# A two-layer hybrid mixer kernel: conditioning loads issued ahead, held subtracts, and six products in the second layer's front

## The chip, the cores and the metric

The kernel runs on one core of one Trainium2 chip. The metric is the device time of one execution in microseconds (us). Before the change it is 1586.25 us, the median of three runs (1586.24 to 1587.02). The engines are called by their short names: PE (TensorE, matmuls), DVE (VectorE), ACT (ScalarE), POOL (GpSimd) and SP (SyncE, which here only issues loads).

## The reference, cut to what matters

256 latent tokens and 256 context tokens of 1024 channels go through two layers. Each layer normalizes, scales and shifts its input by a conditioning vector, projects it once, feeds three mixers from the columns, merges them, and adds an MLP.

```
c_act = silu(c); cc_act = silu(c_ctx)
for l in range(2):
    sh1, sc1, g1, sh2, sc2, g2 = split(c_act @ w_ada[l] + b_ada[l], 6)      # 6144 columns
    ...                                                                      # the same for the context
    h  = rms_norm(x,  norm1[l]) * (1 + sc1)  + sh1
    hc = rms_norm(xc, norm1[l]) * (1 + sc1c) + sh1c
    u_f, dn_qkv, dn_z, dn_ab, da_q, da_k, da_v, gates = split_columns(h @ w_in[l])
    # A: Fourier mixing of u_f; B: bidirectional gated DeltaNet of dn_qkv (conv, silu, chunked delta rule);
    # C: differential attention; merged by sigmoid(gates), projected by w_o
    x = x + g1 * y
    x = x + g2 * squared_relu_mlp(rms_norm(x, norm2[l]) * (1 + sc2) + sh2)
    ...                                                                      # context: layer 0 only
return rms_norm(x, final_norm)
```

## The kernel before, in words

Activations lie channel-major: a tile holds 128 channels by tokens, and k counts the eight channel tiles. Each weight is split into a high and a low part (`whi`, `wlo`) in a rounded 32-bit format, and so is each activation (`hh`, `hl`). One product of 128 output channels is, for each k, three matmuls (`mm3`): high by high, low by high, high by low. A weight chunk is loaded (`raw`), copied by ACT into `whi`, and subtracted by DVE or POOL into `wlo` (`load_w`, L243 to L256).

The program is written with a tile framework that fixes the order on each engine's queue ahead of time: each instruction has a priority, by default its place in the program, and an instruction that the planner holds ready goes ahead of a later one. `Weave.chain` moves work of the mixers to places that are counted in PE's time. A buffer that is used again makes the writer wait for its last reader.

**Front 0** (`front0`, from L1241) prepares layer 0. It forms the square sums of both streams (L1309 on), the norm's row by `norm_rows` (L390: a reciprocal root in small steps, L381 to L387; four diagonal tiles `nd`, L402, that PE turns into rows; copies to `r`), and the conditioning. The first two groups of conditioning columns (shift and scale, eight tiles each) are computed in two ways. For the last NP = 3 tiles of each group PE multiplies (`matvec`): sixteen loads `wn` of 128 x 384 through four buffers. For the others DVE reduces transposed rows (`Rows.step`, L336: two reductions of 1024 elements a row, one for the latent and one for the context vector); the rows come two at a time through a ring of two slots (tile `wv`), and a slot's next load waits until its reductions are done.

Then eight steps follow in the order KO of k. A step finishes the conditioning of its k (two rows, L340, and `mod_gain`, L450), modulates both streams (`modulate`, L453: DVE's product L458, ACT's `hh` L459, ACT's shift L463, and POOL's subtract L464) and adds k to the open products (`step_of`). The products join by JOIN: the gates' 16 columns, then DeltaNet's query and key of head 0, two Fourier gates (C_GF), and DeltaNet's value. A product that joins late catches up on the steps done. All five full-width subtracts of these products are put on POOL by their calls (L1327 to L1331). MV says how many k of `matvec` are done at each step.

**Front 1** (`front1`, L1403) does the same for layer 1, where the conditioning is already there. Three products run along: the gates and DeltaNet's key and value of head 0. It modulates the eight k of the latent stream, then the eight of the context; the context's norm is finished between them. The subtracts of the weights of all twelve DeltaNet chunks of layer 1 alternate between POOL and DVE (`turn_dn`).

Behind each front `mixer` runs the DeltaNet pair of heads 0 and 1 (`dn_pair`): a product, copies by ACT, five taps of a convolution (DVE, L632), tanh, then transposes on PE. Products made in the front are taken from `pre` and not computed again. The Fourier branch follows.

```
places of the loops   KO = [0, 1, 2, 5, 6, 7, 3, 4]      JOIN = [0, 0, 0, 1, 2, 7]
                      MV = [4, 2, 2, 0, 0, 0, 0, 0]      NP = 3
```

Of the kernel before, what the change touches and what calls it, by code (L numbers as in the profile page):

```python
# [19 lines left out]
P = 128  # L20
# [25 lines left out]
NP = 3  # L46
MV = [4, 2, 2, 0, 0, 0, 0, 0]
KO = [0, 1, 2, 5, 6, 7, 3, 4]
JOIN = [0, 0, 0, 1, 2, 7]
# [132 lines left out]
def body(tc, A, dbg=None):  # L182
# [58 lines left out]
    turn_dn = [0]  # L241

    def load_w(l, n, pair=None, eng=V):  # L243
        if l == 1 and n < C_U:

            eng = (G, V)[turn_dn[0] % 2]
            turn_dn[0] += 1
        r = raw_tile(A["wck"][l, n])
        if pair is None:
            hi = wp.tile([P, 1024], F32R, tag="whi", name="whi")  # L250
            lo = wp.tile([P, 1024], F32R, tag="wlo", name="wlo")
        else:
            hi, lo = pair[:, 0], pair[:, 1]
# [20 lines left out]
    def split(src, hi, lo):  # L274
        S.copy(hi, src)  # L275
        V.tensor_tensor(out=lo, in0=src, in1=hi.bitcast(F32), op=ALU.subtract)  # L276
# [35 lines left out]
    class Rows:  # L312
# [15 lines left out]
        def step(self, k=1):  # L328
            for _ in range(k):
# [4 lines left out]
                for v in range(m):  # L334
                    junk = self.pool.tile([P, 1024], F16, tag="junk", name="junk")
                    V.tensor_tensor_reduce(out=junk, in0=r, in1=self.cb[:, v], scale=0.5, scalar=0.0, op0=ALU.mult, op1=ALU.add,  # L336
                                           accum_out=ada[l][:, n, v:v + 1])
# [52 lines left out]
    def norm_rows(ps, rs, pool, pr=None, later=None):  # L390
# [850 lines left out]
    def front0(mp, dp, job, gate_weights):  # L1241
# [5 lines left out]
        pair = lambda pool, tag, dt=F32R: pool.tile([P, 2, 1024], dt, tag=tag, name=tag)  # L1247
        crw = pair(mp, "oD", F32)[0:1].rearrange("p a b -> p (a b)")
# [23 lines left out]
        def wide():  # L1272
            return st.tile([P, 1024], F32, tag="sq", name="sq", bufs=3)

        def add(out, a, b):
            V.tensor_tensor(out=out, in0=a, in1=b, op=ALU.add)

        W = 128 * NP
        pa = [bank("pd") for _ in range(2)]
        mv = [0]  # L1280

        def matvec(m):
            for _ in range(m):
                k = mv[0]
                if k < KT:
                    for i in range(2):
                        r = mp.tile([P, 512], F32, tag="gt", name="wn", bufs=4)[:, :W]
                        nc.sync.dma_start(r, A["wn"][k][:, i * W:(i + 1) * W])
                        PE.matmul(pa[i][0:2, :W], cT[:, k], r, start=k == 0, stop=k == KT - 1)
# [15 lines left out]
        for s in range(2):  # L1305
            tot = st.tile([P, L], F32, tag="mt", name="tot", bufs=3)
            for i in range(2):
                q = wide()
                S.activation(q, x0[s][i].rearrange("p a b -> p (a b)"), AF.Square)  # L1309
                add(q[:, 0:512], q[:, 0:512], q[:, 512:1024])  # L1310
                if i == 0:
                    add(tot, q[:, 0:L], q[:, L:512])
                else:
                    add(q[:, 0:L], q[:, 0:L], q[:, L:512])
                    add(tot, tot, q[:, 0:L])
# [10 lines left out]
        jobs, late = [], [lambda: job("gates", gate_weights(), "pc", 16),  # L1326
                          lambda: job(("dn", 0, 0), load_w(0, C_DN, None, G), "pg"),  # L1327
                          lambda: job(("dn", 0, 1), load_w(0, C_DN + 4, None, G), "pg"),
# [184 lines left out]
```

## Time and profile before

| what | value |
|---|---|
| median of three runs | 1586.25 us |
| time of the profiled execution | 1584.71 us |
| its span, first to last instruction | 1582.6 us |
| PE busy | 1517.0 us, 96% |
| PE weight loads busy | 1305.2 us, 82% |
| DVE busy | 1166.3 us, 74% |
| ACT busy | 735.4 us, 46% |
| POOL busy | 145.0 us, 9% |
| moved by DMA | 215.31 MB, mean 136 GB/s |

Busy times are of one profiled execution. The span is cut into 40 slices of 39.6 us for the rows of tenths. A timeline row merges equal neighbours; its columns are start, length, engine, line, operation, written tile and read tiles, shapes, and count, with the idle time before it and what ended that. A window's row gives each engine's busy time and count, the clock granted to PE as a share of 2.4 GHz, the mean busy share of the DMA engines, and what they moved.

### The profile page before, as it was taken

The page shows a single profiled execution, that of the slowest core. Times are in us where ns is not written, and L with a number is a line of the kernel's source. Part 1 is how long each engine was busy: PE and PEld are TensorE (multiplying, and loading weights), DVE is VectorE, ACT ScalarE, POOL GpSimd, SP SyncE. Part 2 cuts the span into 40 slices and gives each one's busy share as a digit, 9 for nine tenths or more (in the row PEclk, how much of TensorE's full clock was granted, in tenths as well). Part 3 has the DMA queues.
Part 4 walks back from the last instruction along what each step waited for, and adds up shares of the span by engine and source line. Part 5 has one row for each costly group of instructions (what it writes and reads, how often), then busy time and mean ns, then how long its engine had stood idle before and what let it go on. Part 6 is the DMA issues. An engine that isn't in the chain of part 4 may idle for free. (4 is left out here: it accounts for less than half of the span.)

```text
span 1582.6 us, 26109 instructions
## 1 busy us (share of the span) xinstructions
PE 1517.0 (96%) x10114; PEld 1305.2 (82%) x10114; DVE 1166.3 (74%) x2246; ACT 735.4 (46%) x1527; POOL 145.0 (9%) x173
## 2 busy tenths in 40 slices
PE   5899999999999999999999998899999999999997
PEld 2588888777888878888888888888988899999997
DVE  8787774768789797867676755776777886877765
ACT  3475533676532233423223233575457644555543
POOL 3400100011000012000000004001111100100001
PEclk9999999999999999999999999899999999999998
DMA  7532124211257573566566542141332135655662
GB/s 237 192 97 67 35 75 124 82 48 35 80 187 226 189 237 109 164 193 195 181 196 186 186 148 86 56 150 48 111 103 68 42 106 186 188 175 184 190 185 93
DMA packets 64461, 215.31 MB, mean 136 GB/s; under 512 B 7281, under 2 KB 12305, under 8 KB 64081
## 3 DMA queue, kind: packets, MB, share of 16 engines
q1 hardware_dynamic: 58178, 201.96, 40.7%
q10 hardware_dynamic: 5184, 7.21, 1.4%
q0 software_dynamic: 976, 4.48, 1.0%
q8 instruction: 79, 1.29, 0.4%
q14 instruction: 44, 0.36, 0.1%
HBM read 209.42 MB, written 4.20 MB: 135 GB/s over the span
## 5 line engine op out<-in xcount | busy, mean ns | idle before, releaser
L254 ACT CAST whi<-raw 128x1024 fp32r<-128x1024 f32 x277 | 290.5, 1050 | 220.6 <-PE pg L158 98.5
L255 DVE TENSOR_TENSOR wlo<-raw,whi 128x1024 fp32r<-128x1024 f32 x269 | 329.7, 1226 | 80.1 <-ACT whi L254 71.3
L158 PE MATMUL pg<-hh,whi 128*128 128x512 f32 (+1 forms) x856 | 304.0, 355 | 0.2
L158 PE MATMUL pg<-hh,wlo 128*128 128x512 f32 (+1 forms) x856 | 302.9, 354 | 0.5 <-DVE wlo L255 0.5
L158 PE MATMUL pg<-hl,whi 128*128 128x512 f32 (+1 forms) x856 | 303.1, 354 | 0.0
L336 DVE CUSTOM_DVE_ANT_0 junk<-raw,cb 128x1024 f16<-128x1024 f32 x128 | 157.0, 1227 | 57.8 <-DMA raw<-in_wt 56.3
L158 PEld LDWEIGHTS pg<-hh,whi 128*128 128x128 f32 x856 | 162.7, 190 | 20.6 <-issue 0.8
L158 PEld LDWEIGHTS pg<-hl,whi 128*128 128x128 f32 x856 | 162.8, 190 | 19.5 <-issue 0.8
L158 PEld LDWEIGHTS pg<-hh,wlo 128*128 128x128 f32 x856 | 162.7, 190 | 19.1 <-DVE wlo L255 0.7
L158 PE MATMUL pg<-a,whi 128*128 128x256 f32 (+1 forms) x448 | 107.5, 324 | 0.1
L435 POOL TENSOR_TENSOR acc<-acc,sq 128x256 f32<-128x256 f32 x36 | 38.1, 1067 | 661.7 <-ACT sq L433 661.7
L632 DVE SCALAR_TENSOR_TENSOR cy<-cu,conv,cy 128x512 f32<-128x512 f32 (+1 forms) x96 | 69.3, 723 | 30.3 <-ACT cy L630 29.0
L158 PEld LDWEIGHTS pg<-a,whi 128*128 128x128 f32 x448 | 75.8, 188 | 7.7 <-DVE a L276 0.8
L158 PE MATMUL pg<-a,wlo 128*128 128x256 f32 (+1 forms) x224 | 72.1, 322 | 0.0
L878 ACT ACTIVATE gt<-pg 128x256 f32<-128x256 f32 (+1 forms) x43 | 21.0, 488 | 102.6 <-PE pg L158 99.3
L158 PE MATMUL pd<-a,whi 128*128 128x512 f32 (+1 forms) x224 | 56.7, 334 | 0.1
L158 PE MATMUL pa<-hh,whi 128*128 128x512 f32 (+1 forms) x152 | 54.5, 358 | 1.0 <-ACT cy L630 0.9
L158 PE MATMUL pa<-hh,wlo 128*128 128x512 f32 (+1 forms) x152 | 54.0, 355 | 0.0
L158 PE MATMUL pa<-hl,whi 128*128 128x512 f32 (+1 forms) x152 | 53.6, 353 | 0.0
L1235 DVE TENSOR_TENSOR mr<-mr 128x512 f32<-128x512 f32 (+1 forms) x64 | 35.4, 555 | 23.6 <-ACT mr L1234 23.6
L158 PE MATMUL pg<-whi,hh 128*128 128x256 f32 (+1 forms) x160 | 50.9, 318 | 0.7 <-DVE q L996 0.5
L158 PE MATMUL pg<-wlo,hh 128*128 128x256 f32 (+1 forms) x160 | 50.1, 314 | 0.0
(444 smaller groups left out, 3611.4 us busy)
## 6 DMA issues: line engine op xcount, KB each, us to landing
raw<-in_wck SPq DMA_DIRECT2D x280, 512.0 KB, 3.6
raw<-in_wt SPq DMA_DIRECT2D x80, 512.0 KB, 3.6
wv<-in_wt SPq DMA_DIRECT2D x10, 512.0 KB, 4.1
wn<-in_wn SPq DMA_DIRECT2D x16, 192.0 KB, 3.7
x<-in_xin SPq DMA_DIRECT2D x4, 512.0 KB, 8.2
spill<-gt ACTq DMA_DIRECT2D x8, 256.0 KB, 3.9
cb<-crow POOLq DMA_DIRECT2D x2, 1024.0 KB, 7.0
merged<-spill ACTq DMA_DIRECT2D x8, 256.0 KB, 4.6
```

Source lines behind the costliest of these rows:

```text
L158: ins = self.pe.matmul(out, a, b, start=start, stop=stop)
L254: S.copy(hi, r)
L255: eng.tensor_tensor(out=lo, in0=r, in1=hi.bitcast(F32), op=ALU.subtract)
L336: V.tensor_tensor_reduce(out=junk, in0=r, in1=self.cb[:, v], scale=0.5, scalar=0.0, op0=ALU.mult, op1=ALU.add, accum_out=ada[l][:, n, v:v ...
L435: G.tensor_tensor(out=self.acc[s], in0=self.acc[s], in1=q, op=ALU.add)
L632: V.scalar_tensor_tensor(out=y3, in0=u[:, 0:ns, j:j + L], scalar=conv[:, f, j:j + 1], in1=y3, op0=ALU.mult, op1=ALU.add)
L878: S.activation(th, ps[:, :n], AF.Tanh, scale=0.5)
L1235: V.tensor_tensor(out=t, in0=t, in1=t, op=ALU.mult)
```

## The change

In front 0, four tiles of each conditioning group are PE's instead of three, and all sixteen `wn` loads (now 128 x 512) are issued before the norm, each into a buffer of its own: tiles that the later chunk stage of the mixer uses. The loads of x come before the first two rows. The pieces of the square sums are added up less on DVE and more in PE's accumulation. Two products are opened before the norm. Reductions and low-part subtracts that are called after `norm_rows` are ordered behind its last diagonal on DVE's queue (`hold`, `behind`). No subtract is on POOL any more, neither of weights nor of `modulate`. The order of steps and joins is new. In front 1, six products run along the latent stream and four along the context, three of them with weights in tiles of their own.

```diff
-NP = 3
-MV = [4, 2, 2, 0, 0, 0, 0, 0]
-KO = [0, 1, 2, 5, 6, 7, 3, 4]
-JOIN = [0, 0, 0, 1, 2, 7]
+NP = 4
+MV = [5, 3, 0, 0, 0, 0, 0, 0]
+KO = [0, 1, 4, 5, 6, 7, 2, 3]
+JOIN = [0, 0, 1, 2, 3, 4]
...
-    turn_dn = [0]
+    hold = [None]
+
+    def behind(ins):
+        if hold[0] is not None:
+            tc.add_manual_dep(ins.ins, hold[0].ins.name, mybir.DependencyInfo(mybir.DependencyClass.NoSync, mybir.DependencyReason.DATA), reason="behind")
 
     def load_w(l, n, pair=None, eng=V):
-        if l == 1 and n < C_U:
-
-            eng = (G, V)[turn_dn[0] % 2]
-            turn_dn[0] += 1
...
-        eng.tensor_tensor(out=lo, in0=r, in1=hi.bitcast(F32), op=ALU.subtract)
+        behind(eng.tensor_tensor(out=lo, in0=r, in1=hi.bitcast(F32), op=ALU.subtract))
...                                     # the same in split() and for the reductions of Rows.step
-    def norm_rows(ps, rs, pool, pr=None, later=None):
+    def norm_rows(ps, rs, pool, pr=None, later=None, nd=None):
...
-            d = pool.tile([P, P], F32, tag="nd", name="nd", bufs=2)
-            V.tensor_scalar(out=d, in0=one32, scalar1=y[:, t:t + 1], scalar2=None, op0=ALU.mult)
+            d = pool.tile([P, P], F32, tag="nd", name="nd", bufs=2) if nd is None else nd[:, t * P:(t + 1) * P]
+            ins = V.tensor_scalar(out=d, in0=one32, scalar1=y[:, t:t + 1], scalar2=None, op0=ALU.mult)
...
+        return ins
@@ front0
                 nc.sync.dma_start(x0[s][i], A["xin"][s][:, 4 * i:4 * i + 4])
-            if s == 0:
-                aw.fill()
+        aw.fill()
...
+        jobs = [job("gates", gate_weights(), "pc", 16), job(("dn", 0, 0), load_w(0, C_DN), "pg")]
         W = 128 * NP
...
+        places = [(mp, "gt", 4)] * 4 + [(dp, "U32", 3), (dp, "dec", 3)] * 3 + [(dp, "gq", 2)] * 2 + [(dp, t_, 1) for t_ in ("rh", "rl", "T32", "state")]
+        wn = []
+        for k in range(KT):
+            for i in range(2):
+                pool, tag, bufs = places.pop(0)
+                wn.append(pool.tile([P, 512], F32, tag=tag, name="wn", bufs=bufs)[:, :W])
+                nc.sync.dma_start(wn[-1], A["wn"][k][:, i * W:(i + 1) * W])
...                                     # matvec: its loads and their four buffers go
-            tot = st.tile([P, L], F32, tag="mt", name="tot", bufs=3)
+            qs = []
             for i in range(2):
-                q = wide()
+                q = wide() if s + i < 2 else dp.tile([P, 1024], F32, tag="C32", name="sq")
                 S.activation(q, x0[s][i].rearrange("p a b -> p (a b)"), AF.Square)
-                add(q[:, 0:512], q[:, 0:512], q[:, 512:1024])
...                                     # and the adds of the halves into tot
+                V.tensor_tensor(out=q[:, 0:512], in0=q[:, 0:512], in1=q[:, 512:1024], op=ALU.add)
+                qs += [q[:, 0:L], q[:, L:512]]
             for t in range(2):
-                PE.matmul(sums[:, 2 * s + t:2 * s + t + 1], tot[:, t * P:(t + 1) * P], oneD[:, 0:1], start=True, stop=True)
-            if s == 0:
-                aw.step()
-        norm_rows([sums[:, i:i + 1] for i in range(4)], r_, st)
+                for i, q in enumerate(qs):
+                    PE.matmul(sums[:, 2 * s + t:2 * s + t + 1], q[:, t * P:(t + 1) * P], oneD[:, 0:1], start=i == 0, stop=i == 3)
+        aw.step()
+        hold[0] = norm_rows([sums[:, i:i + 1] for i in range(4)], r_, st, nd=dp.tile([P, 512], F32, tag="vn", name="nd"))
...
-                          lambda: job(("dn", 0, 1), load_w(0, C_DN + 4, None, G), "pg"),
-                          lambda: job((C_GF, 1), load_w(0, C_GF + 1, pair(st, "wu"), G), "pa"),
-                          lambda: job((C_GF, 0), load_w(0, C_GF, pair(mp, "oD"), G), "pa"),
-                          lambda: job(("dn", 0, 2), load_w(0, C_DN + 8, pair(st, "wv"), G), "pd")]
+        late = [lambda: job(("dn", 0, 1), load_w(0, C_DN + 4), "pg"),
+                lambda: job((C_GF, 1), load_w(0, C_GF + 1, halves(pair(st, "wu"))), "pa"),
+                lambda: job((C_GF, 0), load_w(0, C_GF, halves(pair(mp, "oD"))), "pa"),
+                lambda: job(("dn", 0, 2), load_w(0, C_DN + 8, (wide(F32R), wide(F32R))), "pd")]
...
-                modulate(0, xv, r_, ma, 0, s, k, st, G)
+                modulate(0, xv, r_, ma, 0, s, k, st)
@@ front1
-        jobs = [job("gates", gate_weights(), "pc", 16)]
-        jobs += [job(("dn", 0, i), load_w(1, C_DN + 4 * i), t_) for i, t_ in ((1, "pg"), (2, "pd"))]
-        for s in range(2):
-            for k in range(KT):
-                modulate(1, x1, r1, ma, 0, s, k, cp_)
-                step_of(jobs, k, s * L, L, X=hs[1])
...
+        with tc.tile_pool(name="st1", bufs=1, reuse_waits="tile") as st:
+            pairs = [[st.tile([P, 1024], F32R, name=f"w{i}{c}") for c in "hl"] for i in range(3)]
+            both = [job("gates", gate_weights(), "pc", 16)]
+            both += [job(("dn", 0, i), load_w(1, C_DN + 4 * i), t_) for i, t_ in ((1, "pg"), (2, "pd"))]
+            lat = [job(("dn", 0, 0), load_w(1, C_DN, pairs[0]), "pg"), job((C_GF, 0), load_w(1, C_GF, pairs[1]), "pa")]
+            both.append(job(("dn", 1, 1), load_w(1, C_DN + 5, pairs[2]), "pa"))
+            for s in range(2):
+                for k in range(KT):
+                    modulate(1, x1, r1, ma, 0, s, k, cp_)
+                    step_of(both if s else both + lat, k, s * L, L, X=hs[1])
...
```

## Rows read from the trace of the kernel before

**Rows 1.** The page: PE's row of busy tenths in 40 slices.
```profile
PE   5899999999999999999999998899999999999997
```
**Rows 2.** Table by windows, front 0.
```profile
0.00:7.30 7.30, 3.50 (x4) 1.49 (x5) 2.44 (x8) 1.50 (x2) 3.69 (x12) 1.00 0.72 155
7.30:13.30 6.00, 3.66 (x6) 1.00 (x4) 4.15 (x9) 4.44 (x8) 0.00 (x0) 1.00 1.02 416
13.30:25.40 12.10, 1.00 (x4) 0.92 (x4) 12.06 (x19) 4.00 (x5) 6.45 (x3) 1.00 0.66 240
...
35.80:82.90 47.10, 41.01 (x167) 25.76 (x166) 33.16 (x59) 21.21 (x43) 20.83 (x18) 1.00 0.56 186
```
**Rows 3.** Timeline of front 0, 16 to 36 us.
```profile
16.82 5.92 POOL L255 TENSOR_TENSOR wlo<-raw,whi 128x1024 fp32r<-128x1024 f32 x2 [2.15 <-ACT whi L254]
...
17.98 2.55 DVE L1276 TENSOR_TENSOR tot<-sq 128x256 f32<-128x256 f32 x1
20.46 2.82 DVE L1276 TENSOR_TENSOR sq<-sq 128x512 f32<-128x512 f32 x1
...
24.35 0.41 DVE L1276 TENSOR_TENSOR sq<-sq 128x256 f32<-128x256 f32 x1
...
28.29 2.27 DVE L383 TENSOR_SCALAR rne<-rne 128x4 f32<-128x4 f32 x1
...
35.77 0.64 PE L158 MATMUL pc<-hh,wab 128*16 128x512 f32 x2
```
**Rows 4.** Timeline of layer 1's front and what follows it.
```profile
974.64 2.32 DVE L387 SCALAR_TENSOR_TENSOR rny<-rnp,rny 128x2 f32<-128x2 f32 x1
...
1016.23 2.33 DVE L530 SCALAR_TENSOR_TENSOR ge<-ge,ge 128x32 f32<-128x32 f32 x1
...
1019.22 1.12 PE L166 MATMUL pc<-kc,cy 128*128 128x128 f32 x4 [3.65 <-DVE cy L637]
```
**Rows 5.** Table by windows, layer 1's front and the convolutions behind it.
```profile
981.70:988.10 6.40, 3.99 (x32) 3.05 (x31) 6.40 (x10) 2.80 (x6) 5.25 (x8) 0.93 0.27 84
988.10:993.80 5.70, 5.70 (x27) 5.07 (x28) 4.27 (x20) 1.84 (x6) 0.00 (x0) 0.50 0.26 92
993.80:1005.60 11.80, 11.79 (x102) 10.82 (x100) 6.52 (x16) 4.48 (x11) 0.00 (x0) 0.99 0.00 0
...
1014.40:1021.60 7.20, 2.34 (x11) 1.57 (x10) 7.20 (x13) 4.40 (x16) 2.90 (x3) 0.74 0.25 71
1021.60:1030.00 8.40, 8.40 (x51) 7.84 (x51) 6.60 (x27) 4.97 (x14) 0.27 (x4) 0.81 0.16 49
```
**Rows 6.** Groups by line on DVE (busy us, mean ns); modulates on the timeline.
```profile
L336 DVE CUSTOM_DVE_ANT_0 junk<-wv,cb 128x1024 f16<-128x1024 f32 x20 | 28.2, 1412 | 2.0 <-DMA wv<-in_wt 1.8
...
L255 DVE TENSOR_TENSOR wlo<-raw,whi 128x1024 fp32r<-128x1024 f32 x2 | 2.4, 1214 | 0.0
...
L336 DVE CUSTOM_DVE_ANT_0 junk<-raw,cb 128x1024 f16<-128x1024 f32 x128 | 157.0, 1227 | 57.8 <-DMA raw<-in_wt 56.3
...
34.26 0.88 DVE L458 SCALAR_TENSOR_TENSOR mt<-x,ma,r 128x256 f32<-128x256 f32 x2 [0.35 <-ACT r L405]
...
996.96 1.27 DVE L461 SCALAR_TENSOR_TENSOR hl<-mt,ada,hh 128x256 fp32r<-128x256 f32 x3
```
**Rows 7.** Timeline: the last square of front 0.
```profile
14.30 1.06 ACT L1309 ACTIVATE sq<-x 128x1024 f32<-128x1024 f32 x1 [0.34 <-DMA x<-in_xin]
```
**Rows 8.** Timeline of PE in front 0.
```profile
26.37 5.24 PE L158 MATMUL pd<-wn,cT 128*2 128x384 f32 x8
...
79.40 0.39 PE L158 MATMUL pg<-hh,whi 128*128 128x512 f32 x1
79.63 0.40 PE L158 MATMUL pg<-hh,wlo 128*128 128x512 f32 x1
...
82.97 0.41 PE L166 MATMUL pd<-kc,ab 16*128 16x16 f32 x4
```
**Rows 9.** Waits of PE, 35 to 115 us: total, times, longest.
```profile
PE pc L158 <- POOL hl L464: 2.1, 3, 0.9
```

More of the change, by code (lines that the diff above doesn't have):

```diff
@@ L252, in load_w @@
         else:
-            hi, lo = pair[:, 0], pair[:, 1]
+            hi, lo = pair
         S.copy(hi, r)
-        eng.tensor_tensor(out=lo, in0=r, in1=hi.bitcast(F32), op=ALU.subtract)
+        behind(eng.tensor_tensor(out=lo, in0=r, in1=hi.bitcast(F32), op=ALU.subtract))
         return hi.rearrange("p (k c) -> p k c", c=P), lo.rearrange("p (k c) -> p k c", c=P)
@@ L275, in split @@
         S.copy(hi, src)
-        V.tensor_tensor(out=lo, in0=src, in1=hi.bitcast(F32), op=ALU.subtract)
+        behind(V.tensor_tensor(out=lo, in0=src, in1=hi.bitcast(F32), op=ALU.subtract))
     cT = cst.tile([P, 8, 2], F32, name="cT")
@@ L335, in step @@
                     junk = self.pool.tile([P, 1024], F16, tag="junk", name="junk")
-                    V.tensor_tensor_reduce(out=junk, in0=r, in1=self.cb[:, v], scale=0.5, scalar=0.0, op0=ALU.mult, op1=ALU.add,
-                                           accum_out=ada[l][:, n, v:v + 1])
+                    behind(V.tensor_tensor_reduce(out=junk, in0=r, in1=self.cb[:, v], scale=0.5, scalar=0.0, op0=ALU.mult, op1=ALU.add,
+                                                  accum_out=ada[l][:, n, v:v + 1]))
     def ada_bias(l, a, b):
@@ L1247, in front0 @@
         pair = lambda pool, tag, dt=F32R: pool.tile([P, 2, 1024], dt, tag=tag, name=tag)
+        halves = lambda t: (t[:, 0], t[:, 1])
         crw = pair(mp, "oD", F32)[0:1].rearrange("p a b -> p (a b)")
@@ L1270, in front0, with wide @@
         r_ = [st.tile([P, L], F32, name=f"r{s}") for s in range(2)]
[L1272 to L1276, printed above, removed]
+        def wide(dt=F32):
+            return st.tile([P, 1024], dt, tag="sq", name="sq", bufs=3)
+        jobs = [job("gates", gate_weights(), "pc", 16), job(("dn", 0, 0), load_w(0, C_DN), "pg")]
         W = 128 * NP
@@ L1286, in matvec @@
                     for i in range(2):
-                        r = mp.tile([P, 512], F32, tag="gt", name="wn", bufs=4)[:, :W]
-                        nc.sync.dma_start(r, A["wn"][k][:, i * W:(i + 1) * W])
-                        PE.matmul(pa[i][0:2, :W], cT[:, k], r, start=k == 0, stop=k == KT - 1)
+                        PE.matmul(pa[i][0:2, :W], cT[:, k], wn[2 * k + i], start=k == 0, stop=k == KT - 1)
                     mv[0] += 1
@@ L1325, in front0 @@
         ma = st.tile([P, 8, 2], F32, name="ma")
-        jobs, late = [], [lambda: job("gates", gate_weights(), "pc", 16),
-                          lambda: job(("dn", 0, 0), load_w(0, C_DN, None, G), "pg"),
-                          lambda: job(("dn", 0, 1), load_w(0, C_DN + 4, None, G), "pg"),
-                          lambda: job((C_GF, 1), load_w(0, C_GF + 1, pair(st, "wu"), G), "pa"),
-                          lambda: job((C_GF, 0), load_w(0, C_GF, pair(mp, "oD"), G), "pa"),
-                          lambda: job(("dn", 0, 2), load_w(0, C_DN + 8, pair(st, "wv"), G), "pd")]
+        late = [lambda: job(("dn", 0, 1), load_w(0, C_DN + 4), "pg"),
+                lambda: job((C_GF, 1), load_w(0, C_GF + 1, halves(pair(st, "wu"))), "pa"),
+                lambda: job((C_GF, 0), load_w(0, C_GF, halves(pair(mp, "oD"))), "pa"),
+                lambda: job(("dn", 0, 2), load_w(0, C_DN + 8, (wide(F32R), wide(F32R))), "pd")]
         for i, k in enumerate(KO):
@@ L1343, in front0 @@
             for s in range(2):
-                modulate(0, xv, r_, ma, 0, s, k, st, G)
+                modulate(0, xv, r_, ma, 0, s, k, st)
             step_of(jobs, k, 0, T, KO)
+        hold[0] = None
         masks()
@@ L1405, in front1 @@
         mod_gain(1, S_N1, 0, ma)
-        jobs = [job("gates", gate_weights(), "pc", 16)]
-        jobs += [job(("dn", 0, i), load_w(1, C_DN + 4 * i), t_) for i, t_ in ((1, "pg"), (2, "pd"))]
-        for s in range(2):
-            for k in range(KT):
-                modulate(1, x1, r1, ma, 0, s, k, cp_)
-                step_of(jobs, k, s * L, L, X=hs[1])
-            if s == 0:
-                norm1.finish(1)
-        cp.__exit__(None, None, None)
+        with tc.tile_pool(name="st1", bufs=1, reuse_waits="tile") as st:
[8 more added lines that the diff above has]
+                    step_of(both if s else both + lat, k, s * L, L, X=hs[1])
+                if s == 0:
+                    norm1.finish(1)
+            cp.__exit__(None, None, None)
     mixer(1, True, front1)
```

5 lines of the change are left out of this document (removed).

## The prediction

> **What bounds the kernel now.** I read the page first, for one question: is TensorE (PE) the engine that sets the time? Its row of tenths has a 9 nearly everywhere, except in the first two slices (5 and 8), slices 25 and 26 (8 each, 950 to 1029 us) and the last one (7) [rows 1]. So outside a few places the time is PE's own work, to which this change adds only the extra columns of the conditioning product. What can be won lies in the first 80 us (front 0) and at the beginning of layer 1 (front 1). A gain there reaches the end undiminished as long as PE is saturated behind it.
>
> Next the table by windows of front 0 [rows 2]. From 13.3 to 25.4 us PE is busy for 1.0 of 12.1 us and VectorE (DVE) for all of it; from 35.8 to 82.9 PE has 167 matmuls in 47.1 us. The timeline says why DVE takes so long [rows 3]: a 256-wide add that takes 0.41 us takes up to 2.55, the next 512-wide one 2.82, and a step of the norm on four columns 2.27. They lie beside subtracts on GpSimd (POOL; 5.92 us for two from 16.82). The first product of the normalized stream starts at 35.77. In layer 1 the same picture is smaller [rows 4]: the last step of `rsqrt_small` on two columns takes 2.32 us, and later a step of the gates 2.33 us, after which PE has stood for 3.65 us waiting for the convolution. The windows there [rows 5] show a second cost: after a stop within 981.7 to 988.1 (PE busy 3.99 of 6.4) the granted clock is 0.50, the lower level of 1.2 GHz, for 5.7 us.
>
> **Front 0.** (1) All full-width subtracts and all second halves of `modulate` leave POOL. On DVE a full-width subtract is 1.21 us, a second half 1.27/3 = 0.42, a first half 0.88/2 = 0.44 [rows 6]. DVE gains five subtracts, 6.1 us, and 16 second halves, 6.8 us. It loses four row reductions: 20 take 28.2 us now [rows 6]; with nothing holding them up, as in the 128 of the later stages (1.23 [rows 6]), and 0.08 for the accumulator's read they are 1.3 each, so 5.2 us. It also loses two 256-wide adds a stream, 4 x 0.41 = 1.6 us, and blocked time: in the norm's chain alone 2.55 - 0.41 = 2.1, 2.82 - 0.6 (half a 1024-wide subtract) = 2.2 and 2.27 - 0.2 = 2.1, together 6.4 us [rows 3]. DVE's work in the whole front is about even, but what lies ahead of the first product is far shorter.
>
> (2) The row loads move behind all four loads of x. The fourth square waits for x until 14.30 us [rows 7]; 1.05 MB less ahead of it at 416 GB/s, the rate from 7.3 to 13.3 us [rows 2], is 2.5 us. ScalarE's four squares (1.06 each [rows 7]) and four tanh need about 6.5 us from 8 us on, so I take 14.0 for the end of the last square, not 15.4. Then an add of 0.7, the rest of the small matmuls 1.5 (PE now sums a stream's four pieces), and the norm's steps, uninterrupted some 4 us (an estimate from the timeline's 0.15 to 0.3 us a step). With half a microsecond for row 0's reductions, which aren't held, the norm's row is there at about 21. Row 8's two reductions (2.6), bias and gain (0.3) and the first modulate (0.9) follow: first product at about 25 us instead of 35.8. The held subtracts and reductions queue on DVE behind four diagonals; who waits for them are PE's products, which need the norm anyway.
>
> (3) That isn't yet the gain, because the second step, k = 1, waits for rows 1 and 9. They are issued only when the ring's two slots come free (about 16 and 23 us), and by then sixteen loads of 256 KB (4.2 MB) and the weights of three further products stand ahead of them on SP's queue. The row that shows what standing behind costs is that of the square at 14.30: its load was issued behind two row loads [rows 7]. By 13.3 us 3.6 MB have moved [rows 2]; the next 7.3 MB at 416 GB/s are in at 31 us; two reductions, bias, gain and modulate put k = 1 on PE at 35 to 37. I take 36. Until then PE has the sixteen conditioning matmuls (5.24/8 x 512/384 = 0.87 us each at the pace of 26.37 [rows 8], 14 us), all with their data by 25 to 27, and k = 0 of all six products.
>
> The Trainium skill, "DMA: Bandwidth & Descriptors", section on queues, rings and completion order, says that on each DMA engine the descriptors of one ring are consumed in ring order, which is against this change, since every row load goes behind the 4.2 MB. By that rule, with which the trace agrees, k = 1 is at 36; if loads shared the engines evenly instead, it would be some 3 to 4 us earlier and the end of the front with it.
>
> (4) From 36 us on seven steps of six products are left. A product's matmuls start every 0.23 us (79.40 to 79.63 [rows 8]), so a step is 6 x 3 x 0.23 = 4.14 and seven are 29 us: 65. DVE has, from 20 us on, 14 reductions (18.3), five subtracts (6.1), 16 modulates (13.8) and biases and gains (2.4): 40.6 us, so its last modulate is at about 61 and PE's last step at 65. Two engines this close cost something in waits: I take 67 for the end of the front, against 82.97 [rows 8]. That is -16. Both bounds: 62 if neither waits and the rows share the queue; 76 if the reductions stay as slow as their present mean of 1.41 us [rows 6] and the row pairs of k = 2 and 3 come late too. So -21 to -7. Behind it DVE will have less rest before the first convolution, and a subtract for the next products comes late: +1.5. **Front 0: -14.5.**
>
> The conditioning's added columns (16 x 0.22 = 3.5 us at the pace of 26.37) and the added small matmuls of the sums (12 x 0.25 = 3 us) lie where PE waits; with that cover gone they cost that much. The loads' buffers are those of the chunk stage, used by nobody before front 0 ends, so they add no wait.
>
> **Front 1.** Without POOL's subtracts the norm's last step loses 2.1 us [rows 4], and PE with it. The stop of 2.4 us in 981.7 to 988.1 goes, and with it 5.7 us at half clock, worth 2.85 [rows 5]: 7.3 us in all. The three added products are 256, 256 and 512 columns: PE's 102 matmuls in 11.8 us [rows 5] give 0.115 us per 256, so 24 x 0.115 x 4 = 11.0 us are done in the front instead of behind it: no change in the sum. Against it stand three more subtracts (3.7 us) that DVE does while it modulates, into buffers that are new there and may be free only when the last product of the MLP has been read. DVE needs about 13 us for eight modulates, subtracts and the second norm, PE 16.5 us for eight steps of six products, so DVE holds, with a start that costs perhaps 1.3. Front: -6.
>
> Behind it the cover is thinner. Now PE has 2.34 us of work in 1014.4 to 1021.6 and 0.81 of its clock until 1030 [rows 5]: 4.9 + 1.6 = 6.5 us lost while DVE runs the convolutions. Afterwards PE has 11 us less to do there, DVE 6 less (the query's convolution, 2.3, fits into the front's second half; three subtracts) and 2.2 less of blocking: 6.5 + 11 - 6 - 2.2 = 9.3 us lost in the worst order, and about 4 if work of the Fourier branch is drawn forward. I take 7.5, so +1. **Front 1: -5**, between -11 and +4.
>
> The query, key and value weights of the second pair also go from POOL to DVE, three subtracts each way of 1.2 against as much blocking: 0, within 2 either way.
>
> **Sum.** -19.5 us on the profiled execution of 1584.7 us (span 1582.6, 2.1 around it), which is 1.5 below the median of 1586.25. On the median 1566.75, rounded to **1567**, with its own range 1561 to 1573.
>
> **Rivals.** A (front 0 half as good): DVE, now with POOL's work, is the bound from 25 to 70 us and the row pairs come late one by one; the front ends at 75, so -8 + 1.5 - 5: 1575. For it: DVE is full from 13 to 25 us [rows 2]; against it: half of that is blocking. B (front 1 gives back): six products leave the convolutions bare, the stop grows and the clock falls again, +3 in place of -5: 1575. For it: the 3.65 us wait is on DVE's chain [rows 4]; against it: 2.2 of it is POOL's doing. C (it doesn't do what it says): the queues hid the norm's delay behind the loads, both fronts end as now: 1585 to 1587. Against it: 6.4 us of DVE standing still. D (better): the rows share the queue, -20 in front 0 and -9 in front 1: 1557.
>
> E (slower): PE's steps of front 0 come apart. From 36 us on DVE feeds PE at its own pace, and if each of the seven steps comes after a stop like the one that in layer 1 took the clock to 0.50 [rows 5], the 29 us of products take 58: the front ends at 94 instead of 83, and with front 1's -5 the kernel is at 1592. It decides if such stops come at every step. Against it: three stops of up to 0.9 us behind POOL's halves [rows 9] left the matmuls at 0.23 us afterwards. The Trainium skill, "TensorE: Matmul & The Clock Gate", section on HAM oscillation, describes such a case, where each wait for data throws the clock back; no run here shows it at every step.
>
> **How the numbers follow.** Forecast 50%, A 19%, B 13%, D 6%, C 5%, E 7%. 0.2% is 3.2 us, about what a measurement of this kernel can tell from no change. Faster by more: forecast, A, B and D, 0.88; within: C, 0.05; slower: E, 0.07. The range runs from 1556, where D lies, to 1581, above A and B and most of both at once; outside are C, E and the tail of D, some 14%.
>
> **What would show it.** Right: first product at 23 to 27 us, k = 1 at 33 to 38, the transposes at 82.97 now at 63 to 72, no step of front 0's norm above 0.4 us on four columns, granted clock 1.00 from 975 to 1005. Step 3 is wrong if rows 1 and 9 land before 28; step 4 if PE stands for more than 5 us in all between 36 us and the front's end; front 1's term if what is lost behind that front is above 10 us. The forecast as a whole is wrong if front 0's end moves by less than 7 us.

## The result, and the profile after

The changed kernel takes 1571.92 us (median of six runs, 1571.45 to 1576.71) against 1585.20 for the kernel before in the same set: ratio 0.9926, 95% interval 0.9913 to 0.9939. The forecast was 1567, with its own range 1561 to 1573. The profiled execution took 1571.99 us with a span of 1570.2, so 12.4 us less than the span of 1582.6.

Where they went is read from starts of the same instruction in both timelines. The transposes that end front 0 start at 76.92 instead of 82.97 [rows 8]: -6.05. ScalarE's last write of the chunk stage's tile `Um` in layer 0 stands at 401.38 instead of 407.49: -6.11, so PE carries the gain on undiminished. Writes of `Um` in layer 1: 1076.03 has become 1068.01 (-8.0), 1115.66 has become 1105.56 (-10.1), and the last but one, at 1274.41, stands at 1262.39 (-12.0). So front 0 gave 6.05 us and layer 1's front with its DeltaNet pairs 5.9. Here are the two pairs of lines that the later sums use, each time before and then after:
```profile
407.49 0.59 ACT L758 CAST Um<-pd 128x512 f16<-128x512 f32 x1 [0.51 <-PE pd L158]
401.38 0.59 ACT L760 CAST Um<-pd 128x512 f16<-128x512 f32 x1 [0.51 <-PE pd L158]
...
1274.41 0.59 ACT L758 CAST Um<-pd 128x512 f16<-128x512 f32 x1 [3.14 <-PE pd L158]
1262.39 0.58 ACT L760 CAST Um<-pd 128x512 f16<-128x512 f32 x1 [3.15 <-PE pd L158]
```
How much the second figure scatters can be read from the runs below: eleven of them, the change among them, have the changed kernel's layer 1, and the time between these two writes lies between 857.5 and 863.6 us in them (mean 861.1; the change 861.0, before 866.9).

PE's row of busy tenths on the page after, answering [rows 1]: the 5 and 8 at the start are 8 and 9, the two 8s at layer 1 are 9s.
```profile
PE   8999999999999999999999999999999999999997
```
The table by windows of front 0 after, answering [rows 2]; k = 1 starts at 46.5, so the last window is cut there.
```profile
13.30:25.40 12.10, 9.53 (x33) 6.51 (x33) 9.14 (x27) 2.55 (x6) 0.53 (x1) 1.00 1.05 390
25.40:35.80 10.40, 10.40 (x25) 2.34 (x24) 8.52 (x18) 1.95 (x3) 0.00 (x0) 1.00 0.86 326
35.80:46.50 10.70, 8.34 (x28) 2.51 (x27) 4.08 (x11) 4.04 (x7) 0.00 (x0) 1.00 0.33 117
46.50:70.00 23.50, 23.50 (x102) 17.51 (x103) 22.21 (x52) 8.70 (x17) 0.00 (x0) 1.00 0.46 163
```
From 13.3 us on PE is busy where it stood before, and from 46.5 on without a gap; DVE does only 4.08 us of work between 35.8 and 46.5.

DVE's timeline after, answering [rows 3].
```profile
18.05 1.22 DVE L337 CUSTOM_DVE_ANT_0 junk<-wv,cb 128x1024 f16<-128x1024 f32 x1
...
20.37 0.17 DVE L384 TENSOR_SCALAR rne<-rne 128x4 f32<-128x4 f32 x1
...
21.57 1.22 DVE L256 TENSOR_TENSOR wlo<-raw,whi 128x1024 fp32r<-128x1024 f32 x1
...
34.29 0.08 DVE L337 DVE_READ_ACCUMULATOR2_ANT ada<- 128x1 f32 x1
42.42 0.17 DVE L1307 TENSOR_TENSOR ada<-pc,sm 128x8 f32<-128x8 f32 x1 [8.05 <-PE pc L166]
42.50 0.15 DVE L341 TENSOR_TENSOR ada<-ada,sm 128x2 f32<-128x2 f32 x1
```
The norm's step on four columns that took 2.27 us takes 0.17. But two instructions of 1.22 us still stand in its chain, and at 34.29, when the last reduction of rows 1 and 9 is done, DVE begins to wait for 8.05 us: next in its queue is the add on the conditioning's result, and k = 1's bias (42.50) stands behind it.

PE's timeline of front 0 after, answering [rows 8].
```profile
10.88 6.99 PE L158 MATMUL pg<-oneD,sq 128*128 128x1 f32 x32
...
24.61 9.43 PE L158 MATMUL pd<-wn,cT 128*2 128x512 f32 x18
33.98 0.64 PE L158 MATMUL pc<-hh,wab 128*16 128x512 f32 x2
...
46.47 0.63 PE L158 MATMUL pc<-hh,wab 128*16 128x512 f32 x2 [1.66 <-ACT hh L461]
...
76.92 0.41 PE L166 MATMUL pd<-kc,ab 16*128 16x16 f32 x4
```
The sixteen fp32 conditioning matmuls are 32 records (so are the sixteen of the sums): one matmul is two records. Eighteen records in a row stand ahead of the first product, which comes at 33.98 although ScalarE has written its operand by 27.7.

Windows of layer 1's front after and what follows, answering [rows 5], and the step of [rows 4] that took 2.32 us.
```profile
970.00:980.00 10.00, 8.68 (x71) 7.83 (x69) 9.23 (x16) 5.68 (x10) 5.21 (x8) 1.00 0.31 107
980.00:990.00 10.00, 9.90 (x82) 9.29 (x81) 10.00 (x29) 5.72 (x14) 0.00 (x0) 1.00 0.49 159
...
1010.00:1020.00 10.00, 6.66 (x33) 5.67 (x32) 9.82 (x23) 6.94 (x19) 0.27 (x4) 0.71 0.13 38
1020.00:1030.00 10.00, 9.90 (x73) 9.02 (x73) 8.45 (x26) 6.41 (x15) 0.13 (x2) 0.95 0.21 60
```
```profile
971.11 0.69 DVE L388 SCALAR_TENSOR_TENSOR rny<-rnp,rny 128x2 f32<-128x2 f32 x1
```
The stop of 981.7 to 988.1 and the lower clock behind it are gone; the one at the convolutions remains: 3.3 us idle, 1.9 by the clock of 0.71, and 0.6 in the next window, 5.9 together.

### The profile page after: what moved, and what is told of

Read it like the earlier page. It is cut to its first block, busy times and chain, and to the rows that moved or that the text cites. A ratio compares the mean times of both kernels' runs of the same rounds, so it can differ in the third digit from the quotient of the medians.

```text
span 1570.2 us, 26157 instructions
## 1 busy us (share of the span) xinstructions
PE 1524.2 (97%) x10164; PEld 1310.9 (83%) x10164; DVE 1156.0 (74%) x2257; ACT 728.2 (46%) x1511; POOL 100.1 (6%) x146
## 5 line engine op out<-in xcount | busy, mean ns | idle before, releaser
L256 DVE TENSOR_TENSOR wlo<-raw,whi 128x1024 fp32r<-128x1024 f32 x274 | 335.2, 1223 | 80.8 <-ACT whi L255 72.0
L255 ACT CAST whi<-raw 128x1024 fp32r<-128x1024 f32 x274 | 287.1, 1049 | 214.0 <-PE pg L158 88.7
L158 PE MATMUL pg<-hl,whi 128*128 128x512 f32 (+1 forms) x848 | 299.2, 353 | 0.0
L158 PEld LDWEIGHTS pg<-hl,whi 128*128 128x128 f32 x848 | 160.1, 189 | 19.5 <-issue 0.8
L880 ACT ACTIVATE gt<-pg 128x512 f32<-128x512 f32 (+1 forms) x42 | 20.6, 490 | 103.9 <-PE pg L158 97.8
L158 PE MATMUL pa<-a,whi 128*128 128x256 f32 (+1 forms) x224 | 52.9, 320 | 0.1
L158 PE MATMUL pa<-hh,wlo 128*128 128x512 f32 (+1 forms) x136 | 49.2, 362 | 0.9 <-DVE wlo L256 0.9
L158 PE MATMUL pg<-whi,hl 128*128 128x256 f32 (+1 forms) x160 | 49.8, 312 | 0.0
```

The costliest lines, as they stand in the source:

```text
L158: ins = self.pe.matmul(out, a, b, start=start, stop=stop)
L256: behind(eng.tensor_tensor(out=lo, in0=r, in1=hi.bitcast(F32), op=ALU.subtract))
L880: S.activation(th, ps[:, :n], AF.Tanh, scale=0.5)
```

## The experiments

### What the gain consists of

**e8: front 0's subtracts on GpSimd (POOL) again.** The five weight subtracts, and the second halves below:
```diff
-                modulate(0, xv, r_, ma, 0, s, k, st)
+                modulate(0, xv, r_, ma, 0, s, k, st, G)
```


> The changed kernel with front 0's five weight subtracts and second halves of modulate on GpSimd again; the loads stay where the change puts them. Theory (front 0's 6 us come from the norm that GpSimd no longer disturbs): a step of the norm on four columns takes over 1 us again, r is copied at 28 to 32 instead of 24.72, the transposes come at 80 to 84 and the kernel at 1575 to 1580. Rival (TensorE is full from 24.6 us on and GpSimd only takes work from VectorE): r moves by 2 to 3 us, k = 1 comes no later than 46.5, the transposes within 1.5 us of 76.92.

1578.69 us (eight runs; 0.9953, 0.9943 to 0.9963), the transposes at 83.37: with the new loads but POOL's subtracts, front 0 gains nothing on before (only its front 0 is read here: the profiled execution, 1584.27, was the longest of the eight). The theory's times for the transposes and the kernel hold, its place only in part: r was to come at 28 to 32. A norm step and a POOL subtract, from the timelines of this run:
```profile
20.99 2.34 DVE L389 SCALAR_TENSOR_TENSOR rnp<-rnp,rne 128x4 f32<-128x4 f32 x1
```
```profile
20.98 2.33 POOL L256 TENSOR_TENSOR wlo<-raw,whi 128x1024 fp32r<-128x1024 f32 x1 [7.06 <-ACT whi L255]
```
DVE's step of 0.16 us ends when POOL's subtract does. That moves r only from 24.72 to 26.01 and k = 1 from 46.47 to 47.73. The other 5.2 of 6.45 us are lost behind k = 1, here a line of PE's timeline and a window of this run:
```profile
55.58 0.40 PE L158 MATMUL pc<-hl,wab 128*16 128x512 f32 x1 [0.90 <-POOL hl L468]
```
```profile
46.50:52.00 5.50, 4.56 (x13) 2.89 (x12) 5.50 (x9) 2.64 (x5) 3.81 (x3) 0.52 0.25 83
```
PE waits for POOL's halves, and its granted clock is 0.52 where the changed kernel has 1.00. The reverse, the kernel before with nothing changed but its subtracts taken off POOL, wasn't run: how much of the 6.45 us needs the new loads and the new order beside it stays open.

The Trainium skill ("SBUF — State Buffer", section on the two separate sides) says that GpSimd and a DVE operation with two SBUF inputs share one port pair, and that whoever comes second is blocked for the other's whole instruction. This trace agrees: 2.34 beside 2.33 us.

**e2: GpSimd back in layer 1** (subtracts of its DeltaNet weights alternate again; six products stay), and **e3: three products in layer 1's front** (GpSimd stays out).
```diff
+        if l == 1 and n < C_U:                      # e2
+            eng = (G, V)[turn_dn[0] % 2]
```
```diff
-                    step_of(both if s else both + lat, k, s * L, L, X=hs[1])      # e3: front1 as before,
+                step_of(jobs, k, s * L, L, X=hs[1])                               # jobs: three products
```


> The changed kernel with the subtracts of layer 1's DeltaNet weights alternating between GpSimd and VectorE again; front 1 keeps its six products. Theory (front 1's gain of 6 us comes from GpSimd's absence beside the norm, not from the products): a step of the second norm on two columns takes 2.3 us again, r1 is copied 2 to 7 us later than 987.4, the granted clock falls below 0.9 somewhere in 980 to 1000, and half of the 6 us or more is lost: span 1573 to 1576. Rival (the three products more bring it): r1 within 1 us of 987.4, span within 1.5 us of 1570.2.

> The changed kernel with layer 1's front as before, three products instead of six; GpSimd stays out. Theory (the gain of layer 1 comes from GpSimd's absence alone, the three products only change places): span within 2 us of the changed kernel's 1570.2. Rival F (the products count: with three, TensorE has 8 x 1.4 us of work beside 13 us of VectorE's and waits): TensorE's waits in 975 to 1010 grow by 4 us or more, the granted clock falls below 0.9 there, span 1573 to 1577. Rival G (six leave the convolutions bare): with three the stop at 1010 to 1020 shrinks by 3 us or more and the span is 1566 to 1568.

e2: 1583.35 us (eight runs; ratio 0.9996, 0.9982 to 1.0010), span 1580.3. The direction of the theory, and more than its figure: r1 is copied at 991.69. Its step of the norm and POOL's subtract, from the timelines:
```profile
969.59 2.31 DVE L394 SCALAR_TENSOR_TENSOR rny<-rnp,rny 128x2 f32<-128x2 f32 x1
```
```profile
969.52 2.37 POOL L260 TENSOR_TENSOR wlo<-raw,whi 128x1024 fp32r<-128x1024 f32 x1 [5.89 <-ACT whi L259]
```
The clock stays at 1.00 in 980 to 1000, where I expected under 0.9; it is at 0.66 later, from 1020 to 1030.

e3: 1568.49 us (two runs; 0.9889, 0.9870 to 0.9909), span 1566.7: 3.5 less than with six products. Rival G has the span right. Layer 1 by itself, from the write of `Um` at 407.5 to the one at 1274.4 (before), as the difference from before's 866.9 us:

| | three products | six products |
|---|---|---|
| GpSimd as before | 0 (before) | +3.1 (e2) |
| GpSimd out | -9.3 (e3) | -5.9 (the change) |

Each cell is one execution. Taking GpSimd out brings 9.0 us with six products and 9.3 with three, and e2's 870.0 us lies 6.4 above the longest of the eleven runs above: this is shown. The three products more cost 3.1 to 3.4 us by the same table, but e3's 857.6 us lies at the lower end of what these eleven show, so the trace alone doesn't tell it from scatter. As a kernel e3 is faster than the change, by intervals that just don't touch (0.9909 against 0.9913). Of G's place for it little shows. The same stop, in e3's windows:
```profile
1000.00:1010.00 10.00, 6.86 (x49) 5.87 (x48) 9.76 (x31) 7.66 (x25) 0.28 (x5) 0.95 0.24 80
1010.00:1020.00 10.00, 10.00 (x57) 8.79 (x56) 8.34 (x25) 6.50 (x17) 0.26 (x4) 0.88 0.29 89
```
It costs 3.1 + 0.3 + 1.2, about 4.7 us, against 5.9. The changed kernel's trace has further waits behind it that e3's lacks, such as 0.9 and 0.6 us for weight halves from 1012 to 1060 and 1.7 for the chunks' `Tm` from 1060 to 1110; whether six products cause them wasn't tried.

### Why front 0 gave 6 us and not 16

All times of this table are read on PE's timelines. (Before had k = 1 early, but a quarter of its conditioning still behind it.) e4 and e14 leave out three quarters of the conditioning product.

| run | first product | k = 1 | last transposes | median, us |
|---|---|---|---|---|
| before | 35.77 | 42.07 | 82.97 | 1585.2 |
| the change | 33.98 | 46.47 | 76.92 | 1571.92 |
| e4: a quarter of the conditioning | 27.66 | 45.09 | 77.37 | 1573.85 |
| e5: DVE's adds behind k = 1 | 29.35 | 47.67 | 80.54 | 1577.52 |
| e6: sums on DVE | 31.23 | 44.37 | 76.55 | 1571.15 |
| e7: all held behind the norm | 32.70 | 47.93 | 80.65 | 1576.84 |
| e13: both queues freed | 29.10 | 43.30 | 75.97 | 1571.68 |
| e14: e13, a quarter | 27.63 | 39.40 | 75.02 | 1571.70 |
| e15: e13, sums on DVE | 27.94 | 38.56 | 71.61 | 1568.84 |
| e17: e15, 384 columns | 28.39 | 38.06 | 71.94 | 1567.36 |
| e19: e17, k = 1 ahead on DVE | 29.54 | 36.11 | 70.88 | 1566.47 |

e2 and e3 have the changed kernel's front 0, and their transposes stand at 76.54 and 75.99. So under about 1 us the last column but one tells nothing (the 18 conditioning records took 9.43 us here, 9.01 and 8.57 there). The medians belong to sets whose runs of before had medians of 1584.57 to 1587.31, so they can be compared only beyond some 3 us.

**e4, e5, e6, e7: one suspect at a time.**
```diff
-                        PE.matmul(pa[i][0:2, :W], cT[:, k], wn[2 * k + i], ...)
+                        if k in (0, KT - 1): PE.matmul(...)               # e4
```
```diff
-            matvec(MV[i])                     # e5: after step_of, and
+                    order(ins, last[0])       # its adds behind k = 1's modulates on DVE
```
```diff
-                    PE.matmul(sums[...], q[...], oneD[:, 0:1], start=i == 0, stop=i == 3)
+                PE.matmul(sums[...], tot[...], oneD[:, 0:1], start=True, stop=True)   # e6: tot is added on DVE
```
```diff
-        jobs = [job("gates", gate_weights(), "pc", 16), job(("dn", 0, 0), load_w(0, C_DN), "pg")]
...
+        hold[0] = norm_rows(...)              # e7: now ahead of the gates, the first weights and row 0
+        jobs = [job("gates", gate_weights(rg), "pc", 16), job(("dn", 0, 0), load_w(0, C_DN, r=r0), "pg")]
         aw.step()
-        hold[0] = norm_rows(...)
```


> The changed kernel with only four of the sixteen conditioning matmuls (k = 0 and 7 of the eight); all sixteen loads stay. It leaves out three quarters of the conditioning product. Theory 1 (TensorE is the bound of front 0 from 24.6 us: the conditioning, two records of about 0.43 to 0.85 us a matmul, stands ahead of the first product): first product at 27 to 29 instead of 33.98, k = 1 at 36 to 38 instead of 46.5, the front's last transposes at 66 to 69 instead of 76.92, some 8 to 11 us less in all. Theory 3 (only the lateness of the norm counts): the norm's row stays at 24.7, the transposes stay within 2 us of 76.9. Rival (VectorE is the bound from 25 us on): k = 1 comes earlier but the transposes stay at 74 or later.

> The changed kernel with the conditioning's two adds of the bias ordered behind k = 1's modulates on VectorE and the conditioning's matmuls behind each step's products in program order; nothing is left out. Theory 2 (the add that waits for the conditioning, with k = 1's bias queued behind it, is what keeps k = 1 from coming at 36): k = 1 at 36 to 38 and the front's transposes at 67 to 70 instead of 76.92. Theory 1 (TensorE is full from 24.6 us to 43.8 anyway): the 8 us of VectorE's wait go, but the transposes come at most 2.7 us earlier, 74.2 to 77.

> The changed kernel with the squares' sums added on VectorE again as in the kernel before (4 small matmuls instead of 16 of two records each). Theory 3 (the norm is late by the small matmuls on TensorE, which end 3.5 us after the last add): the sums are there at 15.5 to 16 instead of 17.87, the norm's row at 22.3 to 23 instead of 24.72, and as the conditioning starts behind the norm's matmuls, the front's transposes at 74.5 to 75. Rival (VectorE is the bound already here): the four added adds of 0.4 us put the norm back by 1.6 us and the gain is under 1 us: transposes at 76 or later.

> The changed kernel with row 0's two reductions and the first two weight subtracts held behind the norm too. Theory 3: the two insertions of 1.22 us (18.05 and 21.57) leave the norm's chain, its row comes at 22.3 instead of 24.72, and the conditioning and all behind it 2.4 us earlier: transposes at 74.5. Rival (what is held back is then late itself): the first modulate waits for row 0's reductions, the first product comes no earlier than 33.98 and the transposes stay at 76 to 78.

All four fail as sole causes, and e5 and e7 end front 0 3.6 and 3.7 us later (as kernels, 0.9943 and 0.9940, their intervals overlap the change's). **e4**: the first product comes at 27.66, as theory 1 says, the end doesn't: its rival's case. The adds on the conditioning's result now stand ahead of the reductions of rows 1 and 9 in DVE's queue: it waits 5.54 us for them, reduces from 33.75 on, and PE, with less to do, stops. From DVE's timeline, e4's table by windows and PE's timeline:
```profile
33.67 0.17 DVE L1308 TENSOR_TENSOR ada<-pc,sm 128x8 f32<-128x8 f32 x1 [5.54 <-PE pc L166]
```
```profile
35.80:46.50 10.70, 5.52 (x11) 2.85 (x12) 10.70 (x25) 3.69 (x7) 0.00 (x0) 0.51 0.70 245
```
```profile
45.92 0.63 PE L158 MATMUL pg<-hh,whi 128*128 128x512 f32 x1
46.35 0.63 PE L158 MATMUL pg<-hh,wlo 128*128 128x512 f32 x1
```
The same product that starts every 0.23 us in the changed kernel starts every 0.43 at a granted clock of 0.51, the lower level.

**e5** didn't take away the wait that it was to take away. ScalarE's and DVE's timelines of this run:
```profile
41.01 0.57 ACT L1305 COPY arow<-pd 2x512 f32<-2x512 f32 x1 [10.67 <-PE pd L158]
41.49 1.04 ACT L258 CAST wu<-raw 128x1024 fp32r<-128x1024 f32 x1
```
```profile
42.56 1.23 DVE L259 TENSOR_TENSOR wu<-raw,wu 128x1024 fp32r<-128x1024 f32 x1 [8.06 <-ACT wu L258]
```
The copy of the conditioning's result holds up ScalarE's queue; the cast of wu stands behind it, and DVE's subtract waits for that cast with k = 1's bias behind it. The same 8 us, through another engine.

**e6**: the sums come no earlier (18.6, not 15.5 to 16), since DVE's own adds are late. But four conditioning matmuls now run ahead of the norm's diagonals, from 18.53 on. PE loses what that gains to k = 1's lateness, a granted clock of 0.76 from 35.8 to 46.5, and this wait of its timeline:
```profile
42.61 0.80 PE L158 MATMUL pa<-hh,wu 128*128 128x512 f32 x1 [2.39 <-DVE wu L256]
```
**e7** has r at 22.54, 2.2 us earlier as theory 3 says, and ends 3.7 us later: a subtract that DVE did at 30.74, ahead of its wait, now comes behind it (40.23), and k = 1 with it.

**e13, e14, e15: the queues of both engines freed**, then less work for PE, or work that starts earlier. As in e5, `matvec` also stands behind each step's products. e14 is e13 with e4's edit, e15 is e13 with e6's.
```diff
-                    S.copy(arow, pa[i][0:2, :W])
+                    order(S.copy(arow, pa[i][0:2, :W]), last[0][0])     # behind k = 1's hh on ACT
+                    order(ins, last[0][1])                              # the add behind its hl on DVE
```


> The changed kernel with everything that waits for the conditioning ordered behind k = 1 on both engines: the copies of its result on ScalarE behind k = 1's hh, the adds of the bias on VectorE behind k = 1's modulates. The earlier run that moved the adds alone still had VectorE waiting 8.06 us, for a cast on ScalarE that stood behind such a copy (10.67 us of wait). Theory 4 (two limits that hide each other: the queues behind the conditioning, and TensorE's own work from 24.6 us on): VectorE's wait of 8 us goes, k = 1's operands are there at 38 to 40, but TensorE stands only 2.4 us between 24.6 and 46.5 in the changed kernel, so the front's last transposes come at 73.5 to 75 instead of 76.92. Theory 2 (the queues alone): 67 to 70. Rival (VectorE's work is the bound, whatever its order): 76 or later.

> The same with only four of the sixteen conditioning matmuls; it leaves out three quarters of the conditioning product. Theory 4: with both limits taken away the front comes down where one alone didn't: k = 1 on TensorE at 38 to 40 and the transposes at 65 to 69. Rival (VectorE's work is the bound): VectorE has some 43 us of work from 18 us on and TensorE follows it by 9 to 11 us: transposes at 70 to 73. If the granted clock falls to 0.50 in TensorE's waits, as it did at 36 to 46 us with the quarter alone, 2 to 4 us more.

> Both queues freed as above and the squares' sums added on VectorE again, so that the conditioning starts on TensorE at 18.5 instead of 24.6 us; nothing is left out. Theory 4: TensorE's work starts earlier and nothing waits for it: the first product at 31, k = 1 at 39 to 41, the transposes at 70 to 73, the kernel 4 to 6 us faster than the changed one, 1566 to 1568. Rival (VectorE's work is the bound): the four adds more on VectorE cost what TensorE gains, transposes at 76 or later, 1571.

**e13**: the waits of PE from 0 to 85 us (total, times, longest) show that hardly anything but the norm's diagonals and the first load holds it up:
```profile
PE pd L158 <- DMA oD<-in_cr: 3.7, 1, 3.7
PE pg L158 <- DVE nd L406: 2.6, 2, 2.0
PE pc L158 <- DVE hl L466: 0.6, 1, 0.6
PE pc L158 <- ACT hh L464: 0.2, 1, 0.2
```
From 24.53 to the transposes at 75.97 PE stands for 0.8 of 51.4 us: there it is the bound. The gain on 76.92 is within the scatter; I had expected 2 to 3.

**e14** ends at 75.02, though k = 1 comes at 39.40. That is outside theory 4's 65 to 69 even with the 2 to 4 us that I had set aside for a lower clock; the rival's 70 to 73 with these 2 to 4 hold it. Of the 51.4 us some 11 of conditioning are gone, but DVE is busy for 14.46 of the 14.92 us from 24.48 to k = 1. So VectorE is a third limit, close behind the other two. PE waits 5.4 us for it and ScalarE there, and then runs slowly:
```profile
35.80:46.50 10.70, 7.99 (x24) 4.80 (x23) 8.17 (x17) 6.54 (x10) 0.00 (x0) 0.63 0.79 276
```
**e15** does what was expected at the front: conditioning from 17.72 on, ahead of the norm's diagonals, transposes at 71.61. As a kernel it takes 1568.84 us (I had put 1566 to 1568; 0.9898, 0.9869 to 0.9927, which still overlaps the change). Against 76.92 the freed queues alone (e13) bring 0.95 us, the earlier start of the conditioning alone (e6) 0.37, both together 5.3.

**e17, e19: both limits moved.**
```diff
-NP = 4                                        # e17: e15 with
+NP = 3
-KO = [0, 1, 4, 5, 6, 7, 2, 3]
+KO = [0, 1, 5, 6, 7, 2, 3, 4]
```
```diff
+            if i == 1:                        # e19: e17, and what is called later goes behind k = 1's multiplications on DVE
+                hold[0] = last[0][1]
```


> The run with both queues freed and the sums on VectorE (transposes at 71.61, span 1567.4), with three of the eight steps' columns from the conditioning product instead of four: 384 columns a matmul, two rows more on VectorE. Nothing is left out. Theory 4 (two limits): the conditioning is 4 us shorter on TensorE, but k = 1 comes when VectorE has it, at 38 to 39 as before, and TensorE then waits: the transposes gain 0 to 1.5 us, 70 to 72. Rival (TensorE alone is the bound by now): 67 to 68.

> The same with the row reductions and weight subtracts of the later steps ordered behind k = 1's modulates on VectorE, so that both limits move. Nothing is left out. Theory 4: k = 1 on TensorE at 35.5 to 37, the transposes at 67 to 70, the kernel at 1563 to 1567 and faster than the changed one by 5 to 9 us. Rival (VectorE's whole work is the bound): k = 1 comes at 36, but the last steps come late and the transposes stay at 71 to 73.

**e17**: a quarter less conditioning alone gives nothing at the front's end, as theory 4 says. PE's timeline:
```profile
38.06 0.64 PE L158 MATMUL pc<-hh,wab 128*16 128x512 f32 x2 [2.50 <-ACT hh L464]
```
**e19** brings k = 1 to 36.11 and the transposes to 70.88, 0.9 short of theory 4's 70 and just under the rival's 71 to 73; against e15 and e17 that is no more than the scatter of about 1 us. PE's timeline shows what the rival says, a stop for the late rows:
```profile
62.06 0.64 PE L158 MATMUL pc<-hh,wab 128*16 128x512 f32 x2 [1.90 <-ACT hh L464]
```
DVE is busy for 10.70 of 10.70 us from 35.8 to 46.5, and PE for 10.39: both are nearly used up. 1566.47 us, ratio 0.9875 (0.9858 to 0.9891); e17 has 1567.36, 0.9881 (0.9867 to 0.9896). Both beat before and the change, whose interval begins at 0.9913; between them no difference can be told. e19 with three products in layer 1 wasn't tried.

## Why the prediction was right in its time and wrong in a term

The sum was -19.5 us, the span moved by -12.4: front 0 gave 6.05 instead of 14.5, layer 1 5.9 instead of 5. The time lies 1.1 us inside the forecast's own range, and that is luck more than mechanism. By its own signs the forecast fails: the first product at 33.98 (23 to 27), k = 1 at 46.47 (33 to 38) and the transposes at 76.92 (63 to 72) all miss, and front 0's end moved by 6.05 us, less than the 7 that it named as the mark of being wrong as a whole. Of its signs of being right two came: no step of front 0's norm on four columns takes DVE more than 0.17 us, and the clock is 1.00 from 975 to 1005. The range was wide enough to hold a front 0 at less than half of what was forecast, because layer 1 came out near its figure.

**Step 1** (VectorE freed of the blocking) was right and is most of the gain: e8 and e2 give all of it back. In front 0 its place was wrong. The norm profits by 1.3 us; 5.2 come from the steps behind k = 1, for which I had counted DVE's work as about even.

**Step 2**: the norm's row at 21 came at 24.72. The added matmuls of the sums, "where PE waits", run until 17.87, 3.5 us behind the last add, where I had 1.5. A row of the timeline counts records, and I had read them as matmuls: the twelve that were added are 24 records of 0.22 us, 5.2 us and not 3. e7 shows 2.2 us for row 0's second reduction and a subtract between norm and diagonals, for which I had set 0.5.

**Step 3 is the one that failed.** Its data came in time: row 1's load landed at 27.5 and row 9's at 30.1, where I had 31 (row 1's was issued ahead of the later weights, at 21.63, not behind them), so its own sign of being wrong, both before 28, didn't show. The rows are reduced at 34.3, and k = 1 could stand at 36: e19, which puts the other reductions and subtracts behind it, has 36.11. Its sentence on PE, "Until then PE has the sixteen conditioning matmuls", 14 us, and "k = 0 of all six products", was never added up: behind a norm at 21 that is 21 + 14 + 4 = 39, not 36. Measured, 15.1 us of conditioning follow the norm at 24.6 (1.87 lay ahead of it), some 4 of k = 0 and 2.4 of waits: 46. So of the 10.5 us by which k = 1 is late, 3 are the sum that wasn't made, 3.6 the late norm of step 2, 2.4 waits, and about 1 a longer conditioning. That the 14 us came out near is luck: two misreadings of [rows 8] cancel. Its x8 are records, four matmuls, so the cost of one was put at half; and they ran at 0.66 us each, where the same records later in the trace of before take 0.34:
```profile
39.40 2.74 PE L158 MATMUL pd<-wn,cT 128*2 128x384 f32 x8
```
Taking the conditioning as something that lies beside waits hid that it is PE's own work. Nor did I ask who stands behind its result: the adds on DVE and the copies on ScalarE hold k = 1's bias back until 42.5. Either limit alone would have set about the same end, so moving one (e13: the queues; e6: PE's start) shows under 1 us, and moving both (e15, e19) gains 5 to 6 us. Taking PE's work away instead (e14) gains only 1.9, since DVE and the lower clock then take over.

**Step 4**: from k = 1 to the end I had 31 us; it took 30.45, and PE stood 2.4 us between 36 and the end. Right, on a start 10.5 late.

**Front 1**: -5 against -5.9, from parts that were both off: the subtracts away from GpSimd bring 9.0 to 9.3 (I had 7.3), the products cost 3.1 to 3.4 by traces that scatter about as much (I had 1.3 in the front and 1 behind it). What is lost behind the front is 5.9 us, not 7.5, and the clock is 1.00 from 970 to 1010, as forecast.

Rival A came nearer to front 0's end (75) but not by its reason: DVE isn't full from 25 to 70 us, it waits for 8. E is refuted: from 46.5 on not one stop.

## What to carry to other kernels

Work that is to fill an engine's wait has to be added up on that engine together with what else is due there, from the first moment at which it can start: 14 us of filling in a gap of 15 leave no room for the next 4. Where early work is put on an engine's queue, look on every other engine for what consumes its result, and keep that behind whatever is due sooner. If taking away either of two suspects changes nothing, take away both before acquitting them, and expect the next limit close behind: here it was the engine that makes the operands.

## What was unexpected of the hardware

Less work on TensorE made its other work slower: with three quarters of the conditioning gone, the same products started every 0.43 instead of 0.23 us (e4 and e14, granted clock 0.51 and 0.63 between 35.8 and 46.5, against 1.00), which in e14 took back 3.4 us (17 products, 0.2 us more each). Ahead of it TensorE had been busy for 9.51 of 14.92 us in e14, where e13 has 18.80 of 18.80 up to its k = 1. An fp32 conditioning matmul of 512 columns is two records, each 0.44 us on average later on (20 in 8.75 us in e13) and 0.93 at the start (2 in 1.87 from 17.80 on in the changed kernel), in windows whose granted clock reads 1.00 throughout; what makes the start slower isn't shown. SP's sixteen loads of 256 KB in a row took 0.85 us each to issue in the changed kernel, where the row load behind them is issued in 0.33, as SP's rows of its timeline show:
```profile
7.63 13.58 SPq L1288 DMA_DIRECT2D wn<-in_wn  x16
21.63 0.33 SPq L326 DMA_DIRECT2D wv<-in_wt  x1
```
